# Two token tiles per step in the gated recurrences of a three-branch mixer, one core

## The chip, the cores and the metric

The kernel runs on one core of a Trainium2 chip. It computes a two-layer model in float32: 256 context tokens and 2,048 latent tokens of width 1,024 go through two layers, each with an input projection, three groups of heads side by side and an output projection. The metric is the device time of one execution in microseconds (us). TensorE (PE in the profile) multiplies, VectorE (DVE) works elementwise, ScalarE (ACT) evaluates functions and copies, GpSimd (POOL) has a few small steps, and SyncE (SP) issues most DMAs. PEld rows are TensorE's weight loads, which overlap its multiplications.

## The reference, cut to what matters

The change lies in the gated recurrences (heads of groups A and C). Per head a state `S` of key width by value width is carried over the tokens, forwards and backwards, in chunks of 64 tokens:

```python
CHUNK = 64
def step(s, inp):                       # one chunk, all heads
    qc, kc, vc, gc = inp
    b = jnp.cumsum(gc, axis=2)          # log decay from the chunk's start
    diff = b[:, :, :, None, :] - b[:, :, None, :, :]
    decay = jnp.where(lower, jnp.exp(jnp.where(lower, diff, 0.0)), 0.0)
    scores = jnp.einsum('bhid,bhjd,bhijd->bhij', qc, kc, decay)
    o = (jnp.einsum('bhij,bhjv->bhiv', scores, vc)
         + jnp.einsum('bhid,bhdv->bhiv', qc * jnp.exp(b), s))
    b_end = b[:, :, -1:, :]
    s = (s * jnp.exp(b_end[:, :, 0, :])[..., None]
         + jnp.einsum('bhjd,bhjv->bhdv', kc * jnp.exp(b_end - b), vc))
    return s, o
...
o_lf, _ = scan_dir(lat, 0, s_cf)        # forwards, from the context's final state
o_lb, _ = scan_dir(lat, 1, s_cb)        # backwards
return o_lf + o_lb, o_ctx
```

Group A has 4 heads with 64 keys, group C 4 heads with 32 keys; all values are 64 wide. Group B is latent attention with 4 heads over all 2,304 tokens. The outputs of the three groups are gated, joined and projected; the second layer needs no context output.

## The kernel before

The program is laid out by a scheduler that takes the operations in the order in which the Python code writes them as their priority and fixes, ahead of time, one order of instructions for each engine. Tiles come from pools by tag; `bufs` says how many buffers a tag has, and a new tile of a tag waits until the oldest is no longer read.

Each layer has three stages. `project` (to about 700 us in the first layer, from about 1,800 to 2,620 us in the second) multiplies the normed tokens with twelve groups of weights and stores the results in DRAM: forget gates `F`, keys `K` and queries `Q` with the key dimension on partitions, values and gates in `nat` by token. `mix` (about 700 to 1,750 us and 2,620 to 3,640 us) holds the attention and the recurrences side by side. `output` projects.

In `mix`, two generators are advanced in turn. `attention` yields after each pair of heads of a 128-token tile. The recurrence has two sweeps over 18 tiles of 128 tokens: `back_states` goes backwards and stores the backward scan's state at each chunk's end in `sb`; `recur` goes forwards and makes the outputs. `mix` advances the recurrence in proportion to the attention done; a tile of `recur` counts as 2.5 tiles of `back_states`, and a tile is written out whole.

All heads lie in three blocks of 128 rows: two blocks of group A (64 rows per head) and one of group C (32 rows per head, four heads). `fa`, `ka` and `qs` hold decays, keys and queries of a tile for both directions. The scores of a chunk are worked out in levels: level -1 is the diagonal, and levels 0 to 5 join neighbouring runs of 1 to 32 tokens. For each level, ScalarE gathers the keys (`km`, L706), TensorE multiplies keys and queries (`pa`, L774), VectorE merges the result under a mask into `acc` (L779), and VectorE multiplies keys (`ka`, L716, L719) and queries (`qa`, L728, L739) by the decays of the neighbouring runs and joins the decays (`t`, L741).

`level_scores` gives TensorE 12 products per tile and level. Each uses 64 rows and 64 columns of the array, at position (0, 0) or (64, 64) in turn: eight of 64 moving columns (group A) and four of 128 (group C). Since a block of 64 rows holds two heads of group C, their queries are stored twice in `Q`, each copy with the other head's rows at zero (L474), so one product with 128 columns serves both heads. A product on 32-bit operands shows as two records in the trace.

`chunk_products` turns the keys (`pk`, L614), copies them (`kn`, L616) and multiplies by the values (`pub`, `puf`, L623), 16 products per tile into two PSUM tiles, one per chunk. `chunk_outputs` adds 48 products per tile into two PSUM tiles `po`, one per half of the heads (L790, L801), at four positions of 64 by 64 if both halves run together. All of `pa`, `pub`, `puf` and `po` share the PSUM tag `R` with two buffers of one bank each.

Of the kernel before, what the change touches and what calls it, by code (L numbers as in the profile page):

```python
# [7 lines left out]
F32 = mybir.dt.float32  # L8
# [8 lines left out]
P = 128  # L17
# [11 lines left out]
SEG = 128  # L29


def view(ap, offset, dims, parts=None):
    """A free-dimension pattern of its own on the tile behind ap."""
    pd = list(ap.ap[0])
    if parts is not None:
        pd[1] = parts
    return bass.AP(ap.tensor, ap.offset + offset, [pd] + [list(d) for d in dims])


class Route:  # L40
    """Tiles by tag, each from the pool that holds the tag: the order of pools is the order in memory."""
# [12 lines left out]
class Trunk:  # L54
    def __init__(self, ctx, tc, io, nlat):
# [5 lines left out]
        self.ntiles = self.nt // P  # L61
        self.cpool = ctx.enter_context(tc.tile_pool(name="cpool", bufs=1))
# [10 lines left out]
    def split(self, hi, lo, src, hi_eng="act", lo_eng="dve"):  # L73
        """src = hi + lo with both parts in the tensor engine's one-pass format."""
# [10 lines left out]
    def rsqrt(self, pool, v, n, name):  # L85
        """(v + eps already added) ** -0.5 for a [P, n] tile."""
# [4 lines left out]
    def constants(self):  # L91
# [3 lines left out]
        self.mhalf = c.tile([P, 8], F32, name="mhalf")  # L95
        nc.vector.memset(self.mhalf, -0.5)
        # the gated heads' query scale, on the rows of the even and of the odd heads
        self.hm = c.tile([P, 2], F32, name="hm")
        for r in range(4):
            for i in range(2):  # L100
                nc.vector.memset(self.hm[32 * r:32 * r + 32, i:i + 1], float(32.0 ** -0.5) if r % 2 == i else 0.0)
# [7 lines left out]
    def scratch(self, l):  # L109
        """Layer l's arrays in DRAM, and its modulation columns."""  # L110
# [5 lines left out]
        S["F"] = d.tile([P, self.ntiles, 2, 3, SEG], F32, name=f"dF{l}")  # L116
        S["K"] = d.tile([P, self.ntiles, 2, 3, SEG], F32, name=f"dK{l}")
        S["Q"] = d.tile([P, self.ntiles, 4 * SEG], F32, name=f"dQ{l}")
# [4 lines left out]
        S["sb"] = d.tile([P, self.ntiles, 2, 3, 64], F32, name=f"dsb{l}")  # L123
# [12 lines left out]
    def mod_first(self, S, R, ps, first):  # L136
        """Layer 0's shift and scale as columns."""
# [23 lines left out]
    def mod_rest(self, S0, S1, R, bm0):  # L161
        """Layer 0's gate and layer 1's modulation: products along the free dimension, one column block at a time."""
# [41 lines left out]
    def lower_bounds(self, S):  # L204
        """Layer 1's forget-gate floor: the running sum of the softmax over layers less its first term."""
# [20 lines left out]
    def gate_weights(self, l, S, R):  # L226
        """The low-rank gate weights stacked [hi; hi; lo], against gates stacked [hi; lo; hi]."""
# [9 lines left out]
    def latent_weights(self, l, S, R, ps):  # L237
        """The low-rank query and key weights joined: M_h = W_uq,h W_uk,h^T; and the rotary and value ones."""
# [38 lines left out]
            # the first two weight groups run side by side while the first block's tokens come in  # L277
# [59 lines left out]
    # weight groups in the order in which they run: first column, number of columns  # L337
# [17 lines left out]
    def normed_pair(self, l, S, R, ps, pr, plain=False):  # L355
        """The modulated norm of two token tiles, transposed: [d, k, 256]; plain leaves out the modulation."""
# [47 lines left out]
    def group(self, l, S, R, ps, g, w, h, pairs):  # L404
        """One weight group against a block's token pairs; yields after each pair."""
# [4 lines left out]
        def natural(pr):  # L410
            """[P, tile of the pair, 256]: tokens on partitions, n weight columns."""
# [9 lines left out]
        def transposed(pr):  # L421
            """[P, 128-column block, 256]: weight columns on partitions, the pair's tokens."""
# [12 lines left out]
        def by_tile(o):  # L435
# [758 lines left out]
```

## Time and profile before

| | us |
|---|---|
| median of 3 runs | 3836.99 |
| lowest and highest | 3836.19, 3838.03 |
| span of the profiled execution | 3840.8 |
| TensorE busy in it | 3740.7 (97%) |
| VectorE busy | 2529.3 (66%) |
| ScalarE busy | 1452.2 (38%) |

The page gives each engine's busy time, its busy share in 40 slices, and the granted clock of TensorE. A matmul's row shows how long it was in the array, and matmuls overlap, so the busy time of PE says only that something was in flight; what a piece of work costs PE is read from the starts of the rows: the start of the next piece less its own. The timeline of an engine merges neighbouring rows of one line, with the count behind the x.

### The profile page before, as it was taken

How to read it: one execution, taken by the hardware profiler on the slowest of the kernel's cores; microseconds unless marked ns; L12 is line 12 of the kernel's file. 1: busy time of each engine (PE TensorE's matmuls, PEld its weight loads, DVE VectorE, ACT ScalarE, POOL GpSimd, SP SyncE). 2: the span in 40 equal slices, each digit the busy share in tenths (PEclk: the TensorE clock that was granted, in tenths of full speed). 3: DMA queues.
4: the chain of work that ended last, by engine and by line, in shares of the span. 5: the costliest groups of instructions: out<-in, count | busy, mean ns of one | idle time of the engine just before them, and what ended most of it. 6: DMA issues, size and time to landing. Idle time of an engine off the chain costs nothing.

```text
span 3840.8 us, 82784 instructions
## 1 busy us (share of the span) xinstructions
PE 3740.7 (97%) x34152; PEld 3341.4 (87%) x34152; DVE 2529.3 (66%) x6956; ACT 1452.2 (38%) x2347; POOL 187.3 (5%) x194
## 2 busy tenths in 40 slices
PE   8899999999999999998999999999999999999899
PEld 5899999888888888887879999998888888888777
DVE  6763242577888888776765432426778888888566
ACT  3524242344444444442115252523444444444400
POOL 1000000000000000010110000000000000000111
PEclk9999999999999999999999999999999999999999
DMA  7775453323222212114435453523231212211232
GB/s 253 229 206 155 122 155 108 110 85 92 76 68 62 69 57 69 54 59 167 150 105 181 141 156 101 170 90 118 78 96 49 79 55 69 73 55 33 89 140 104
DMA packets 305850, 415.30 MB, mean 108 GB/s; under 512 B 43008, under 2 KB 235840, under 8 KB 304448
## 3 DMA queue, kind: packets, MB, share of 16 engines
q1 hardware_dynamic: 304032, 407.64, 33.8%
q8 instruction: 269, 4.41, 0.5%
q10 hardware_dynamic: 1440, 2.36, 0.2%
q14 instruction: 109, 0.89, 0.1%
HBM read 290.89 MB, written 119.03 MB: 107 GB/s over the span
## 4 chain that ended last, share of the span: by engine, by line
PE 71%; DVE 2%; DMA 2%; ACT 1%; issue 0%; POOL 0%; SPq 0%; DVEq 0%; ACTq 0%; POOLq 0%
PE pj L417 10%; PE pa L774 7%; PE ptp L924 6%; PE pj L428 5%; PE oc L917 4%; PE oc L913 4%; PE pzo L1069 3%; PE pzo L1070 3%; PE pzo L1071 3%; PE pss L888 3%; PE oc L914 3%; PE pss L889 3%; PE pss L891 3%; PE pss L890 3%; PE pss L892 3%; PE po L801 1%
## 5 line engine op out<-in xcount | busy, mean ns | idle before, releaser
L417 PE MATMUL pj<-wh,hl 128*128 128x256 f32 (+1 forms) x2224 | 623.0, 281 | 8.4 <-DVE hl L83 8.4
L417 PE MATMUL pj<-wh,hh 128*128 128x256 f32 (+1 forms) x2224 | 624.5, 281 | 2.0 <-DVE ve L369 1.2
L417 PE MATMUL pj<-wl,hh 128*128 128x256 f32 (+1 forms) x2224 | 623.1, 280 | 0.0
L77 ACT CAST ph<-ptp 128x512 fp32r<-128x512 f32 x580 | 333.2, 586 | 369.9 <-PE ptp L924 349.6
L83 DVE TENSOR_TENSOR pl<-ptp,ph 128x512 fp32r<-128x512 f32 x580 | 392.9, 686 | 111.2 <-ACT ph L77 109.9
L893 DVE TENSOR_SCALAR_CACHE_REDUCE sx<-pss 128x512 f32<-128x512 f32 (+1 forms) x648 | 399.2, 631 | 79.5 <-PE pss L892 74.2
L417 PEld LDWEIGHTS pj<-wh,hl 128*128 128x128 f32 x2224 | 421.5, 190 | 9.3 <-DVE hl L83 9.3
L417 PEld LDWEIGHTS pj<-wh,hh 128*128 128x128 f32 x2224 | 423.1, 190 | 2.7 <-DVE ve L369 1.6
L417 PEld LDWEIGHTS pj<-wl,hh 128*128 128x128 f32 x2224 | 422.3, 190 | 0.0
L924 PE MATMUL ptp<-ident,sx 128*128 128x128 f32 x2320 | 368.5, 275 | 17.2 <-ACT sx L903 17.2
L903 ACT ACTIVATE sx<-sx,nm 128x2304 f32<-128x2304 f32 (+1 forms) x136 | 288.4, 2121 | 173.5 <-DVE nm L899 171.4
L913 PE MATMUL oc<-ph,cnh 128*128 128x256 f32 x1160 | 346.0, 320 | 5.1 <-ACT ph L77 4.4
L83 DVE TENSOR_TENSOR wl<-wraw,wh 128x1024 fp32r<-128x1024 f32 (+1 forms) x144 | 169.6, 1211 | 238.8 <-ACT wh L77 238.7
L428 PE MATMUL pj<-hh,wh 128*128 128x256 f32 x1136 | 321.0, 283 | 0.0
L428 PE MATMUL pj<-hh,wl 128*128 128x256 f32 x1136 | 319.3, 281 | 0.0
L428 PE MATMUL pj<-hl,wh 128*128 128x256 f32 x1136 | 318.2, 280 | 0.0
L914 PE MATMUL oc<-ph,cnl 128*128 128x256 f32 x1160 | 301.9, 282 | 0.0
L924 PEld LDWEIGHTS ptp<-ident,sx 128*128 128x128 f32 x2320 | 272.8, 141 | 28.0 <-ACT sx L903 19.4
L774 PE MATMUL pa<-qa,km 64*64 64x64 f32 (+1 forms) x4896 | 279.3, 248 | 3.4 <-DVE qa L739 3.1
L888 PE MATMUL pss<-cth,qh 128*128 128x512 f32 (+1 forms) x648 | 269.4, 416 | 5.4 <-DVE sx L893 5.0
L917 PE MATMUL oc<-pl,cnh 128*128 128x256 f32 x1160 | 251.1, 297 | 7.0 <-DVE pl L83 6.8
L774 PEld LDWEIGHTS pa<-qa,km 64*64 64x64 f32 x4896 | 202.4, 134 | 58.4 <-issue 34.3
(241 smaller groups left out, 8035.7 us busy)
## 6 DMA issues: line engine op xcount, KB each, us to landing
wraw<-in_w_in_dram SPq DMA_DIRECT2D x132, 512.0 KB, 4.7
dnat<-stg SPq DMA_DIRECT2D x104, 256.0 KB, 2.1
vg<-dnat SPq DMA_DIRECT2D x34, 512.0 KB, 4.2
yt<-dy SPq DMA_DIRECT2D x34, 512.0 KB, 3.6
wmt<-in_w_modT_dram SPq DMA_DIRECT2D x64, 256.0 KB, 4.0
fa<-dF SPq DMA_DIRECT2D x36, 384.0 KB, 3.3
ka<-dK SPq DMA_DIRECT2D x36, 384.0 KB, 3.3
dK<-stg SPq DMA_DIRECT2D x36, 256.0 KB, 4.1
```

The source lines that it names most:

```text
L77: nc.scalar.copy(hi, src)
L83: nc.vector.tensor_tensor(lo, src, hi, op=ALU.subtract)
L417: nc.tensor.matmul(pj[:, j, :n], h[pr][a][:, k, tk], w[b][:, k, :n], start=(k == 0 and a + b == 0), stop=(k == KD - 1 and a == 1))
L428: nc.tensor.matmul(pj[:, j, :], w[b][:, k, cs], h[pr][a][:, k, :], start=(k == 0 and a + b == 0), stop=(k == KD - 1 and b == 1))
L774: nc.tensor.matmul(pa[rows, po:po + n], km[rows, sl, tk:tk + 64], mv, start=True, stop=True, tile_position=(64 * e, 64 * e))
L888: nc.tensor.matmul(pss[:, :n], G["qh"][hp][:, i, tk], K["cth"][:, ks], start=True, stop=False)
L893: nc.vector.tensor_scalar(sx[:, ks], pss[:, :n], SCALE, None, op0=ALU.mult, op1=ALU.max, accum_out=mx[:, nb:nb + 1])
L903: nc.scalar.activation(sx[:, :nk], sx[:, :nk], AF.Exp, bias=nm, accum_out=sm)
L913: nc.tensor.matmul(oc, K["cnh"][:, ks], ph[:, c, :], start=(kc + c == 0), stop=False)
L914: nc.tensor.matmul(oc, K["cnl"][:, ks], ph[:, c, :], start=False, stop=False)
L917: nc.tensor.matmul(oc, K["cnh"][:, ks], pl[:, c, :], start=False, stop=(kc + c == nch - 1))
L924: nc.tensor.transpose(pt[:, c, i, :], pexp[i][:, (kc + c) * P:(kc + c + 1) * P], self.ident)
```

## The change

Every step of the recurrences takes two token tiles (a pair, 256 tokens, four chunks). `F`, `K`, `Q` and `sb` are stored by pairs. The directions in `F` change places, so that one vector instruction per level reaches both directions: `qa` is made by one product instead of four, and each level's products on `qa` by one instruction instead of four to six. `ka`, `t`, the merge and the sums cover 256 tokens. Tags that had two buffers (`fa`, `ka`, `vg`, `qs`, `acc`, `v2`, and in the attention `ym`) have one of twice the size; `R` is one PSUM tile of two banks. `Q` holds group C's queries once, scaled; the copies with zeros, `qm`, are made by ScalarE just before the outputs. In `level_scores` the products of group C use 32 rows at positions (0, 0), (64, 64), (32, 0) and (96, 64) with 64 moving columns; group A's products of a level come first, then group C's. `recur` yields after each level, an eighth of 2.5 each time.

```diff
-SEG = 128
+SEG = 256
+NCH = SEG // 64
...
             elif g == 5:
-                o, o2 = stage(), stage()
-                for i in range(2):
-                    nc.scalar.mul(view(o[:], 64 * i, [[SEG, 4], [1, 64]]),
-                                  pj[:, 0].rearrange("p (c n) -> p c n", n=64), self.hm[:, i:i + 1])
-                nc.sync.dma_start(out=S["Q"][:, tt, 2 * SEG:4 * SEG], in_=o)
-                nc.scalar.copy(o2[:, 1], pj[:, 1])
+                o = stage()
+                nc.scalar.mul(o[:, 0], pj[:, 0], float(32.0 ** -0.5))
+                nc.scalar.copy(o[:, 1], pj[:, 1])
+                nc.sync.dma_start(out=S["Q"][:, pr, 2, :], in_=o[:, 0])
...
+    def chunk_products(self, rp, rps, kT, vt):
+        nc = self.nc
+        kn = rp.tile([P, 2, 3 * P], F32, tag="km", bufs=2, name="kn")
+        for j in range(2):
+            pk = rps.tile([P, 3, P], F32, tag="mi", name="pk")
+            for b in range(3):
+                nc.tensor.transpose(pk[:, b, :], kT[:, b, j * P:(j + 1) * P], self.ident)
+            nc.scalar.copy(kn[:, j], pk.rearrange("p b n -> p (b n)"))
+        pu = rps.tile([P, 2, 512], F32, tag="R", name="pu")
+        for j in range(2):
+            for s in range(4):
+                for e, c in ((0, 0), (1, 1), (1, 0), (0, 1)):
+                    ksl, rows, blk, vb = self.head_rows(4 * e + s)
+                    cs = slice(64 * c, 64 * c + 64)
+                    o = 192 * j + 64 * blk
+                    nc.tensor.matmul(pu[rows, c, o:o + 64], kn[cs, j, ksl], vt[cs, j, vb * 64:vb * 64 + 64],
+                                     start=True, stop=True, tile_position=(64 * c, rows.start))
+        return pu[:, :, 0:384].rearrange("p c (j n) -> p c j n", j=2)
+
+    def advance(self, to, st, tt, ch, pu):
         for b in range(3):
...
+            self.nc.vector.scalar_tensor_tensor(
+                out=to[:, b, :], in0=st[:, b, :], scalar=tt[:, b, ch:ch + 1],
+                in1=pu[:, ch % 2, ch // 2, b * 64:b * 64 + 64], op0=ALU.mult, op1=ALU.add)
...
+                qa = rp.tile([P, 2, L3], F32, tag="qa", name="qa")
+                nc.vector.tensor_tensor(qa, qs.rearrange("p b n -> p (b n)").unsqueeze(1).to_broadcast([P, 2, L3]),
+                                        fa.rearrange("p d b n -> p d (b n)"), op=ALU.mult)
...
+                if need:
+                    km = rp.tile([P, 3, SEG], F32, tag="km", bufs=2, name="km")
+                    for d in range(2):
+                        blk = [[2 * c, nb], [1, c]]
+                        nc.scalar.copy(view(km[:], c * d, blk), view(kap, L3 - d * (L3 - c), blk))
+                    self.level_scores(rps, km, qa, c, lv, acc)
...
                 if need:
-                    # d = 0: suffix products of the backward decays; d = 1: prefix products of the forward ones
-                    qap = qa[:]
-                    nq = SEG // (2 * c)
-                    for d in range(2):
-                        q0 = d * (L4 + c)
-                        tb = lt + 1 if d == 0 else 0
-                        qv = view(qap, q0, [[2 * c, 2 * nq], [1, c]])
-                        nc.vector.tensor_tensor(qv, qv, view(tap, tb, [[2, 2 * nq], [0, c]]), op=ALU.mult)
...
-                        for pt in parts:
-                            qv = view(qap, q0 + pt[0], pt[1:4])
-                            nc.vector.tensor_tensor(qv, qv, view(tap, tb + pt[4], pt[5:8]), op=ALU.mult)
...
+                    qv = view(qa[:], 0, [[2 * c, nb], [L3 + c, 2], [1, c]])
+                    nc.vector.tensor_tensor(qv, qv, view(tap, 1, [[2, nb], [lt - 1, 2], [0, c]]), op=ALU.mult)
...
+                if need:
+                    yield 2.5 / 8
...
     def level_scores(self, rps, km, q, c, lv, acc):
...
-        pa = rps.tile([P, 512], F32, tag="R", bufs=2, name="pa")
...
+        pa = rps.tile([P, 2, 512], F32, tag="R", name="pa")
+        todo = []
+        for ch in range(NCH):
+            tk = slice(64 * ch, 64 * ch + 64)
+            for sl in range(4):
+                n, b = (64, sl) if sl < 2 else (32, 2)
                 for e in range(2):
...
+                    r = 64 * e if sl < 2 else 64 * e + 32 * (sl - 2)
+                    rows = slice(r, r + n)
...
+                    po = 128 * ch + 64 * (sl // 2)
+                    todo.append((sl // 2, pa[64 * e:64 * e + 64, sl % 2, po:po + 64], km[rows, b, tk], mv, (r, 64 * e)))
+        for part in range(2):
+            for g, out, w, mv, pos in todo:
+                if g == part:
+                    nc.tensor.matmul(out, w, mv, start=True, stop=True, tile_position=pos)
...
     def chunk_outputs(self, S, rp, rps, p, acc, qa, v2, vt, sbt, sts):
...
+        qm = []
+        for i in range(2):
+            m = rp.tile([P, 2, SEG], F32, tag="km", bufs=2, name="qm")
+            nc.scalar.mul(m, qa.rearrange("p d (b n) -> p d b n", b=3)[:, :, 2], self.hm[:, i:i + 1])
+            qm.append(m)
+        po = rps.tile([P, 2, 512], F32, tag="R", name="po")
...
-            total = self.ntiles * (1 + self.PACE)
+            total = self.npairs * 3.5
```

First place: TensorE, outputs of one step of `recur` in the first layer. `po` are the output products, `puf` chunk products, `ptp` and `oc` attention. Before:

```order
L924 MATMUL ptp<-ident,sx 128x128 x6
L623 MATMUL puf<-vg,kn 64x64 x4
L623 MATMUL puf<-vg,kn 32x64 x4
L790 MATMUL po<-v_12886,acc 64x64 x8
L801 MATMUL po<-sbt,qa 64x64 x2
L801 MATMUL po<-stf,qa 64x64 x2
```

After:

```order
L914 MATMUL oc<-ph,cnl 128x256
L789 MATMUL po<-v_12044,acc 64x64 x32
L801 MATMUL po<-sbt,qa 64x64 x4
L801 MATMUL po<-stc,qa 64x64
```

Where a tile's outputs came in two halves of 24 products with attention between them, a pair's 96 products stand in one row.

Second place: TensorE, one level's product `pa` among attention (`pss`, `oc`, `ptp`, `poa`) in the first layer. Before:

```order
L924 MATMUL ptp<-ident,sx 128x128 x6
L774 MATMUL pa<-qs,ksum 64x64 x8
L774 MATMUL pa<-qs,ksum 64x128 x4
L892 MATMUL pss<-ks,rl 128x512
L888 MATMUL pss<-cth,qh 128x512
```

After, one product whole, and one in pieces:

```order
L936 MATMUL poa<-uv_1137,os 128x128 x2
L765 MATMUL pa<-qa,km 64x64 x32
L888 MATMUL pss<-cth,qh 128x512
L889 MATMUL pss<-ctl,qh 128x512
```

```order
L765 MATMUL pa<-qa,km 64x64 x13
L917 MATMUL oc<-pl,cnh 128x256 x2
L765 MATMUL pa<-qa,km 64x64 x7
L888 MATMUL pss<-cth,qh 128x512
```

A tile's 12 products have become a pair's 32, all of 64 columns, and there are half as many levels; some are still cut by attention products.

Third place: VectorE, one level in the first layer (`qa`, `ka`: queries and keys; `acc`: the merge; `pl`, `sx`: attention). Before:

```order
L728 TENSOR_TENSOR qa<-qa,t_17143 128x64x2
L739 TENSOR_TENSOR qa<-qa,t_17143 128x32x2
L779 COPY_PREDICATED acc<-mask,pa 128x512
L739 TENSOR_TENSOR qa<-qa,t_17143 128x32x2 x3
L716 TENSOR_TENSOR ka<-ka,t_17193 128x24x2x8
```

After:

```order
L769 COPY_PREDICATED acc<-mask,pa 128x1024
L724 TENSOR_TENSOR qa<-qa,t_17926 128x48x2x8
L717 TENSOR_TENSOR ka<-ka,t_18008 128x24x2x16
L893 TENSOR_SCALAR sx,mx<-pss 128x512
L85 TENSOR_TENSOR pl<-ptp,ph 128x512
```

The merge of a pair now comes first, then one product on `qa`; `ka` runs two levels ahead.

## Rows read from the trace of the kernel before

**Rows 1.** The page: busy us, share, instructions; granted clock in 40 slices.

```profile
PE 3740.7 (97%) x34152; PEld 3341.4 (87%) x34152; DVE 2529.3 (66%) x6956; ACT 1452.2 (38%) x2347; POOL 187.3 (5%) x194
PEclk9999999999999999999999999999999999999999
```

**Rows 2.** Windows, both mixes: us, busy us of each engine, clock, DMA, GB/s.

```profile
700.00:1700.00 1000.00, 983.58 (x10706) 837.87 (x10705) 815.26 (x2628) 432.74 (x694) 31.20 (x34) 1.00 0.24 72
2620.00:3600.00 980.00, 965.46 (x10199) 825.88 (x10199) 786.26 (x2513) 428.58 (x667) 34.69 (x33) 1.00 0.23 70
```

**Rows 3.** Waits of PE, whole span: us in total, times, longest.

```profile
PE oc L917 <- DVE pl L83: 6.8, 14, 1.6
...
PE pa L774 <- DVE qa L739: 3.1, 3, 2.4
```

**Rows 4.** Timeline of PE, one level product: start, us, what, count [idle before].

```profile
931.70 0.40 PE L917 MATMUL oc<-pl,cnh 128*128 128x256 f32 x2
932.03 1.12 PE L774 MATMUL pa<-qs,ksum 64*64 64x64 f32 x24
933.08 0.39 PE L838 MATMUL pq<-cqh,mh 128*128 128x256 f32 x1
933.30 0.28 PE L838 MATMUL pq<-cql,mh 128*128 128x256 f32 x1
933.42 0.27 PE L838 MATMUL pq<-cqh,ml 128*128 128x256 f32 x1
```

**Rows 5.** Timeline of PE, outputs of one tile, both halves together.

```profile
1223.59 0.40 PE L917 MATMUL oc<-pl,cnh 128*128 128x256 f32 x2
1223.83 0.49 PE L924 MATMUL ptp<-ident,sx 128*128 128x128 f32 x3
1224.25 0.70 PE L790 MATMUL po<-v,acc 64*64 64x64 f32 x32
...
1225.58 0.30 PE L801 MATMUL po<-stf,qa 64*64 64x64 f32 x8
1225.82 0.33 PE L924 MATMUL ptp<-ident,sx 128*128 128x128 f32 x1
```

**Rows 6.** Timeline of PE, outputs of one tile, one half alone.

```profile
1291.94 0.68 PE L790 MATMUL po<-v,acc 64*64 64x64 f32 x16
...
1293.49 0.39 PE L913 MATMUL oc<-ph,cnh 128*128 128x256 f32 x1
```

**Rows 7.** Timeline of PE, chunk products of one tile, whole, then one half.

```profile
907.38 0.73 PE L623 MATMUL pub<-bv,kn 64*64 64x64 f32 x32
908.04 0.55 PE L614 MATMUL pk<-ident,bk 128*128 128x128 f32 x3
...
910.82 0.69 PE L623 MATMUL pub<-bv,kn 64*64 64x64 f32 x16
911.44 0.39 PE L913 MATMUL oc<-ph,cnh 128*128 128x256 f32 x1
```

**Rows 8.** The page's groups: level products 0 to 5 (count, busy, mean ns, idle).

```profile
L774 PE MATMUL pa<-qa,km 64*64 64x64 f32 (+1 forms) x4896 | 279.3, 248 | 3.4 <-DVE qa L739 3.1
```

**Rows 9.** Groups of VectorE by form: busy us, mean ns of one, idle before.

```profile
L779 DVE COPY_PREDICATED acc<-mask,pa 128x512 f32<-128x512 uint8 x204 | 150.4, 737 | 13.5 <-PE pa L774 12.9
L739 DVE TENSOR_TENSOR qa<-qa,t 128x64 f32<-128x64 f32 x544 | 96.4, 219 | 0.9 <-PE pa L774 0.8
L728 DVE TENSOR_TENSOR qa<-qa,t 128x128 f32<-128x128 f32 x340 | 85.0, 287 | 16.1 <-PE pa L774 15.3
L716 DVE TENSOR_TENSOR ka<-ka,t 128x384 f32<-128x384 f32 x136 | 75.4, 554 | 13.4 <-ACT km L706 13.2
...
L716 DVE TENSOR_TENSOR ka<-ka,fa 128x384 f32<-128x384 f32 x34 | 29.5, 869 | 0.0
```

**Rows 10.** Timeline of PE, a level product that waits.

```profile
945.03 1.12 PE L774 MATMUL pa<-qa,km 64*64 64x64 f32 x24 [2.36 <-DVE qa L739]
```

**Rows 11.** The page's DMA issues: count, KB each, median us to landing.

```profile
ka<-dK SPq DMA_DIRECT2D x36, 384.0 KB, 3.3
```

More of the change, by code (lines that the diff above doesn't have):

```diff
@@ L691, in recur @@
                 ksum = rp.tile([P, 3, SEG], F32, tag="km", bufs=2, name="ksum")
                 nc.vector.tensor_tensor(ksum, ka[:, 0], ka[:, 1], op=ALU.add)
-                acc = rp.tile([P, 512], F32, tag="acc", bufs=2, name="acc")
-                v2 = rp.tile([P, 2, 256], F32, tag="v2", bufs=2, name="v2")
-                for e in range(2):
-                    nc.sync.dma_start(out=v2[64 * e:64 * e + 64],
-                                      in_=S["nat"][tk, 256 * e:256 * e + 256].rearrange("(c j) n -> j c n", c=2))
@@ L698, in recur @@
[L698 to L710 removed]
+                acc = rp.tile([P, 2, 512], F32, tag="acc", name="acc")
@@ L711, in recur @@
+                self.level_scores(rps, ksum, qs, 1, -1, acc)
+                yield 2.5 / 8
+            ta = fa
+            for lv in range(6):
+                c = 1 << lv
                 nb = L3 // (2 * c)
@@ L784, in chunk_outputs @@
+    def chunk_outputs(self, S, rp, rps, p, acc, qa, v2, vt, sbt, sts):
         nc = self.nc
-        po = [rps.tile([P, 256], F32, tag="R", bufs=2, name="po") for _ in range(2)]
-        quads = ((0, 0), (1, 1), (1, 0), (0, 1))
-        for sl in range(4):
-            for e, c in quads:
-                rows = slice(64 * e, 64 * e + 64)
-                nc.tensor.matmul(po[e][64 * c:64 * c + 64, sl * 64:sl * 64 + 64],
-                                 acc[rows, c * 256 + sl * 64:c * 256 + sl * 64 + 64],
-                                 v2[rows, c, sl * 64:sl * 64 + 64], start=(sl == 0), stop=False,
-                                 skip_group_check=True, tile_position=(64 * e, 64 * c))
@@ L804, in chunk_outputs @@
-        o = rp.tile([P, 512], F32, tag="o", bufs=2, name="o")
-        for e in range(2):
-            nc.scalar.copy(o[:, e * 256:e * 256 + 256], po[e])
-        sq = rp.tile([P, 512], F32, tag="sq", name="sq")
-        nc.scalar.activation(sq, o, AF.Square)
-        ss = rp.tile([P, 8], F32, tag="rss", bufs=2, name="rss")
+                    o = 256 * j + 64 * sl
+                    oa = 128 * (2 * j + c) + 64 * (sl // 2)
+                    nc.tensor.matmul(po[64 * c:64 * c + 64, e, o:o + 64], acc[rows, sl % 2, oa:oa + 64],
+                                     v2[rows, 2 * j + c, sl * 64:sl * 64 + 64], start=(j == 0 and sl == 0), stop=False,
+                                     skip_group_check=True, tile_position=(64 * e, 64 * c))
@@ new lines, in chunk_outputs @@
+        for j in range(2):
+            for sl in range(4):
+                for d in range(2):
+                    for e, c in quads:
+                        rows = slice(64 * e, 64 * e + 64)
+                        ch, b, o = 2 * j + c, min(sl, 2), 256 * j + 64 * sl
+                        tk = slice(64 * ch, 64 * ch + 64)
+                        q = qm[sl - 2][rows, d, tk] if sl > 1 else qa[rows, d, sl * SEG + 64 * ch:sl * SEG + 64 * ch + 64]
+                        sv = sbt[rows, ch, b, :] if d == 0 else sts[ch][rows, b, :]
+                        nc.tensor.matmul(po[64 * c:64 * c + 64, e, o:o + 64], q, sv, start=False,
+                                         stop=(d == 1 and sl == 3 and j == 1), skip_group_check=True,
+                                         tile_position=(64 * e, 64 * c))
@@ L819, in query_group @@
+        nc.sync.dma_start(out=self.pair_rows(S["y"], p, 0, 512), in_=o)
     def query_group(self, S, ap, aps, t):
@@ L1096 @@
     CHEAP = 0.3
-    PACE = 2.5
     EARLY = 1000
```

269 lines of the change are left out of this document (110 added, 159 removed).

## The prediction

> **What bounds the kernel now.** I read the page first. TensorE is busy for 97% of the span, VectorE for 66%, ScalarE for 38%, and the granted clock is 1.00, the 2.4 GHz level, in all slices that do work [rows 1]. The share alone says little, since matmuls overlap, so the windows come next: in the steady part of both mixes TensorE has something in flight for 98% of the time, at clock 1.00, and VectorE works for 80 to 82% [rows 2]. Last come the waits. The only ones that TensorE has on the recurrence in any number are three of 3.1 us in all, and on the attention's subtraction `pl` 14 of 6.8 us [rows 3]. So the mixes are bound by TensorE's stream. An edit is worth what it takes out of that stream, and VectorE's saved time is worth nothing until TensorE waits for it. The change can therefore gain in one way (a recurrence that costs TensorE less) and lose in one (a longer chain from VectorE back to TensorE).
>
> **Prices of TensorE's small tiles.** They come from starts, not durations. One level product has 24 records: 16 of 64 columns and 8 of 128, which is 32 widths of 64. In [rows 4] its first record starts at 932.03 and the next line at 933.08, so it takes 1.05 us, with two array positions in turn. Half a tile's outputs (48 records of 64) takes 1293.49 - 1291.94 = 1.55 us, also with two positions [rows 6]. The difference, 0.50 us for 16 widths, is **31 ns per width with two positions**, and 1.05 - 32 x 0.031 leaves 0.06 us for the batch itself. All 96 records at four positions take 1225.82 - 1224.25 = 1.57 us [rows 5], so (1.57 - 0.06) / 96 = **15.7 ns per width with four positions**. A change between full tiles and small ones costs something too. Two `oc` records take 0.33 us ahead of a small batch [rows 4] and 0.24 ahead of full ones [rows 5]: 0.09 to enter. The record behind a small batch takes 0.22 instead of the 0.12 of its kind (933.08 to 933.30 and to 933.42 [rows 4]): 0.10 to leave. **A batch costs 0.19 us beside its own time.** The chunk products fit the prices: whole, 32 records take 908.04 - 907.38 = 0.66 us, and half of them 911.44 - 910.82 = 0.62 [rows 7]. For the whole batch 32 x 0.0157 + 0.06 = 0.56, so 0.10 is left, which I put on the change of tile height inside it (64 to 32 rows).
>
> **The change on TensorE, term by term.**
>
> Level products. [rows 8] has 4,896 records, so 34 tiles by 6 levels by 24; with the diagonal there are 34 x 7 = 238 products, and 17 x 7 = 119 for pairs. Two tiles cost 2 x 1.05 = 2.10 us now. For a pair, group A has 32 records at two positions, 32 x 0.031 = 0.99; group C has 32 records that may run at four positions, 32 x 0.0157 = 0.50; with 0.06 for the batch and 0.10 for the change of height that is 1.65. No row shows a level product with tiles of 32 rows. The bounds of group C's half are 0.50 and 0.99, and I take 0.50, because in the outputs [rows 5] four positions of which two share their columns already run at that price. 119 x 0.45 = **-53 us**.
>
> Batches. Counting small tiles that follow one another as one batch, the trace of before has 452 and the new order has 338: 114 x 0.19 = **-22 us**.
>
> Outputs. Of 34 tiles 16 have them whole and 18 in halves: 16 x 1.57 + 18 x 3.10 = 81 us. After, all 17 pairs have one run of 192: 17 x (192 x 0.0157 + 0.06) = 52. **-29 us**.
>
> Chunk products. There are 72 now (18 tiles in each layer and sweep); 44 are whole and 28 in halves: 44 x 0.66 + 28 x 1.24 = 64 us. After there are 36 of twice the size, and at most the whole price for each half of one: 72 x 0.66 = 48. **-16 us**.
>
> Cut products. Attention cuts 98 of the 238 level products now, and 59 of 119 in the new order. Their entering and leaving is in the batches; beyond that a piece may leave a position idle. If a cut costs 14 widths of 0.031 us more than now in each of the 59, that is +26 us, and as much less is as possible. I take 0 and keep +-26 for the range.
>
> **The change on VectorE and the chain back.** VectorE's products have one price: 64 elements 219 ns, 128 elements 287, 384 elements 554 [rows 9], so about 150 ns and 1.05 ns per element. The new merge has 1,024 elements. Its bounds are one and two of today's 737 ns; I take 737 + 512 x 1.05 = 1.27 us. The new `qa` product has 768: 150 + 768 x 1.05 = 0.95 us (bounds 0.55 and 1.11; with the pattern of level 0, which takes 869 ns for 384, up to 1.74). In all VectorE loses instructions; that is hidden by the same stream of TensorE that hides them today, and its value is 0.
>
> What does count is that `R` now is one PSUM tile. The next level's product starts only when the merge has read the last one, and when `qa` is multiplied, and the order puts these behind one another: 1.27 + 0.95, with 0.27 for the last record's way through the array [rows 4] and half a microsecond for an attention operation that VectorE has just begun, about 3.0 us. Behind a waiting product stands all of the attention, since TensorE's order is fixed. Today the same wait exists and costs up to 2.36 us in a place [rows 10], but rarely, as two tiles of `R` let the merge lag. From the new order, with the times of the rows above, I added up the attention that lies between one level's product and the next: 102 steps, median 3.4 us, mean 4.0, fifteen of them under 2.0. The part of the chain that is not covered sums to 17 us for a chain of 2.6, 29 for 3.2, 82 for 4.0, 124 for 4.6 and 157 for 5.0. For 3.0 I take **+25 us**.
>
> **At nothing.** ScalarE makes two `qm` per pair more and copies the same keys; it is at 43% in the mixes [rows 2]. SyncE issues fewer transfers. `fa`, `ka` and `vg` have one buffer now, so the next pair's loads start when this pair is through with them: 768 KB for `fa` and `ka`, by 3.3 us for 384 KB [rows 11] 6.6 us. In the new order 10 to 45 us of other products lie between a pair's last level and the next pair's first, which covers it; if that cover were gone, 17 x 5 = 85 us would be the most. The projection has the same matmuls and drops one stored segment of `Q`. The recurrence still ends about two attention steps ahead of the attention, so no tail appears.
>
> **Sum.** -53 - 22 - 29 - 16 + 25 = -95 us. On the profiled execution's 3840.8 that is 3745.8; the profiled execution lies 3.8 us above the median of the runs, so the median should be **about 3740**.
>
> **Rivals.** *Only two of the 32-row products run at a time.* Two of the four positions share an output bank of `pa` in different rows of the array; should that, or tiles of 32 rows, stop them from overlapping, group C costs 31 ns per width: 119 x 32 x 0.0153 = +58 us, 3798. For it speaks that no row has this tile; against it that today's two positions, which also write one bank, already overlap at 31 ns a width [rows 4] and would otherwise need twice that. The Trainium skill, "TensorEngine Tiling (Array Packing)", section "Restrictions and Gotchas", Gotcha 1, says that tiles in different rows of the array cannot use the same PSUM bank at the same time. By it today's level product would take about 2.05 us where the trace has 1.05, so here the trace disagrees with it for tiles that write different partitions, and no run shows it for 32 rows. Chance 0.18.
>
> *The chain becomes the bound, and the kernel is slower.* Place: between `pa` of one level and of the next, where VectorE's attention operations (a `copy_predicated` of 512 elements, 737 ns, is about their size [rows 9]) get between merge and `qa`, two or three of them each time, and the chain is 5.0 us. Price 157 instead of 25: 3740 + 132 = 3872. It decides from a chain of 4.6 us, where 124 us eat the whole gain of 120. For it speaks that VectorE is the second busiest engine in the mixes [rows 2]; against it that the order has merge and `qa` behind one another in most steps and that VectorE gets idler. Chance 0.09.
>
> *No change.* A chain between 4.4 and 4.6: 0.03. *A deeper gain*: cuts at -26 and the chain well covered, 17 us or less: 3705; chance 0.07.
>
> **How the numbers follow.** The forecast, 3740, has the remaining 0.63, with a range of its own of 3710 to 3770 (cuts +-26, merge and `qa` at their bounds). The range of 3703 to 3800 adds the rival of the 32-row tiles and the deeper gain, and leaves the slower and unchanged cases and some edges out. A measurement of this kernel tells about 0.2%, 7.7 us, from no change. Faster: 0.63 + 0.18 + 0.07 = 0.88; same 0.03; slower 0.09.
>
> **What would show it.** Starts of `pa`: a whole batch of 64 records 1.65 us long, its second half 0.5 against 1.0 for the first; 2.15 in all would show the first rival. 192 records of `po` in 3.07 us. Some 340 small batches. A steady VectorE share well under 80%. In the waits of TensorE, `pa` on `acc` or `qa` with some 25 us; over 120 there would prove the second rival, and waits of `pa` on a load or on `fa` would show that single buffers are not free. If all four terms are there and the time is not, the recurrence no longer fits beside the attention, and the gap is a tail at the end of a mix.

## The result and the profile after

The changed kernel takes 3866.34 us (median of three runs, 3866.07 to 3869.9) against 3836.99: 1.0075 of the time before, 95% interval 1.0057 to 1.0093. It is slower by 29 us where the prediction had 97 us faster. The profiled execution's span is 3864.6 us. The page's busy times and granted clock:

```profile
PE 3665.0 (95%) x36056; PEld 3309.4 (86%) x36056; DVE 2418.7 (63%) x5430; ACT 1437.7 (37%) x2296; POOL 185.3 (5%) x159
PEclk9999999999999999998999999999999999999999
```

TensorE is in use for 76 us less than in [rows 1] and VectorE for 111 us less, yet the span is longer: the work went down and the waiting went up. The windows of both mixes show it (us, busy us of PE, PEld, DVE, ACT, POOL, granted clock, DMA share, GB/s); the same windows before are [rows 2]:

```profile
700.00:1700.00 1000.00, 939.10 (x11507) 817.38 (x11507) 751.83 (x1813) 426.64 (x674) 28.55 (x19) 0.98 0.22 69
2620.00:3600.00 980.00, 920.31 (x11039) 801.25 (x11039) 729.19 (x1772) 416.04 (x642) 28.56 (x19) 0.98 0.22 67
```

TensorE was in use for 983.58 and 965.46 us there and is for 939.10 and 920.31 now, and the mean clock fell from 1.00 to 0.98. What TensorE waits for (total, times, longest; what answers to [rows 3]):

```profile
PE oc L917 <- DVE pl L85: 51.7, 31, 4.7
PE pss L888 <- DVE sx L893: 22.2, 21, 3.8
PE oc L913 <- ACT ph L79: 21.9, 22, 2.3
...
PE pa L765 <- DVE qa L724: 12.3, 16, 2.8
```

The first three are the attention's instructions: its products on `pl` and `ph`, and its scores `pss`, which need VectorE to have read the last ones (`sx`). Before, they waited 6.8 us [rows 3] and

```profile
PE pss L888 <- DVE sx L893: 5.0, 7, 1.5
PE oc L913 <- ACT ph L77: 4.4, 6, 1.5
```

The recurrence's own product `pa`, on which the prediction had set its 25 us, waits 12.3 for `qa`.

Adding up TensorE from each record's start to the next record's start (or to its own end, if nothing follows at once), over both mixes, gives the account. The third kernel is run r5 below, the fourth r15.

| us in both mixes, rounded | before | after | one tile, r5 | pairs, work left out, r15 |
|---|---|---|---|---|
| recurrence (`pa`, `po`, `pu`) | 445 | 344 | 358 | 362 |
| attention (`pss`, `oc`, `ptp`, `poa`) | 1470 | 1493 | 1464 | 1486 |
| other products | 109 | 111 | 107 | 109 |
| idle | 46 | 141 | 41 | 79 |
| sum | 2070 | 2089 | 1970 | 2035 |

So the recurrence gave back 101 us, idle time took 95 of them, the attention's own records took 23 more, and the other stages 5. (r5's sum is 119 us under that of the changed kernel; another 18 us between these two lie outside the mixes, and no run looks into those.)

**The terms on TensorE came out.** A whole level product of a pair, and the one of r5 for one tile (timelines of TensorE: start, us, what, count):

```profile
1427.34 1.77 PE L765 MATMUL pa<-qa,km 64*64 64x64 f32 x64 [0.39 <-DVE qa L724]
1429.04 0.50 PE L888 MATMUL pss<-cth,qh 128*128 128x512 f32 x1
```

```profile
986.56 1.07 PE L773 MATMUL pa<-qa,km 64*64 64x64 f32 x32
987.56 0.38 PE L896 MATMUL pss<-cth,qh 128*128 128x256 f32 x1
```

From start to next start that is 1.70 us for a pair (1.65 was forecast, 2 x 1.05 before) and 1.00 for a tile. The 16 widths of each group between the two cost 0.70. The single records in the trace show how: in the first part two records start 7 to 36 ns apart, in the second four within 20 ns, and in both the next such set follows 58 ns after the last. That is 29 ns per width in group A and 15 in group C, and 8 x 58 + 4 x 58 ns is the 0.70.

**Where the idle time arises.** At the end of a pair, VectorE, ScalarE and TensorE of the changed kernel:

```profile
1303.92 1.11 DVE L726 TENSOR_TENSOR t<-t 128x192 f32<-128x192 f32 x4
1305.63 1.23 DVE L814 TENSOR_TENSOR o<-o,rrs 128x1024 f32<-128x1024 f32 x1 [0.59 <-POOL rrs L90]
1306.89 1.23 DVE L815 TENSOR_TENSOR o<-o,vg 128x1024 f32<-128x1024 f32 x1
1308.03 0.95 DVE L717 TENSOR_TENSOR ka<-ka,t 128x768 f32<-128x768 f32 x1
1308.90 0.69 DVE L85 TENSOR_TENSOR pl<-ptp,ph 128x512 fp32r<-128x512 f32 x1
```

```profile
1304.46 0.59 ACT L79 CAST ph<-ptp 128x512 fp32r<-128x512 f32 x1 [0.94 <-PE ptp L924]
```

```profile
1304.62 0.28 PE L914 MATMUL oc<-ph,cnl 128*128 128x256 f32 x1
1309.64 0.79 PE L917 MATMUL oc<-pl,cnh 128*128 128x256 f32 x2 [4.74 <-DVE pl L85]
1310.23 0.41 PE L924 MATMUL ptp<-ident,sx 128*128 128x128 f32 x1
...
1310.66 0.41 PE L914 MATMUL oc<-ph,cnl 128*128 128x256 f32 x1
```

`ph` is there at 1305.05, so `pl` could start. In VectorE's fixed order the products with the norm and with the gates (L814, which waits another 0.59 us for GpSimd's power, and L815) and the next pair's `ka` stand in front of it: 3.85 us from 1305.05 until `pl` starts at 1308.90. TensorE's order has nothing between the products on `ph` and those on `pl`, so it stands still for 4.74 us.

**What a wait costs beyond itself.** Behind it, L914 takes 0.41 us instead of 0.28. The window names the clock:

```profile
1309.60:1313.00 3.40, 3.36 (x11) 2.98 (x12) 1.80 (x5) 1.01 (x1) 0.00 (x0) 0.50 1.01 312
1320.00:1330.00 10.00, 9.58 (x170) 8.56 (x169) 9.97 (x22) 5.64 (x9) 0.00 (x0) 1.00 0.41 134
```

0.50 is the lower level, 1.2 GHz. In the mixes of the changed kernel 20 stretches of 2 to 9 us have records of the longer kind, 85 us in all, against 7 with 28 us before. At half the pace 57 us more of it cost up to 29 us. By the granted clock, 80 us of the attention's own time lie at 0.50, against 24 before; half of the 56 us more is 28, so the clock is all of the attention's 23 us, and without it the attention would take some 5 us less than before.

### The profile page after: what moved, and what is told of

The parts are those of the page before. It is cut to its first block, busy times and chain, and to the rows that moved or that the text cites. A ratio compares the mean times of both kernels' runs of the same rounds, so it can differ in the third digit from the quotient of the medians.

```text
span 3864.6 us, 84193 instructions
## 1 busy us (share of the span) xinstructions
PE 3665.0 (95%) x36056; PEld 3309.4 (86%) x36056; DVE 2418.7 (63%) x5430; ACT 1437.7 (37%) x2296; POOL 185.3 (5%) x159
## 4 chain that ended last, share of the span: by engine, by line
PE 46%; DVE 5%; DMA 2%; issue 1%; POOL 1%; ACT 1%; SPq 0%; DVEq 0%; ACTq 0%; POOLq 0%
PE pj L420 10%; PE pj L431 5%; PE pzo L1070 3%; PE pzo L1071 3%; PE pzo L1072 3%; PE ptp L924 3%; PE pa L765 2%; PE oc L917 2%; PE pss L888 2%; PE oc L913 2%; PE pss L889 1%; PE pss L890 1%; PE pss L891 1%; PE pss L892 1%; PE oc L914 1%
## 5 line engine op out<-in xcount | busy, mean ns | idle before, releaser
L914 PE MATMUL oc<-ph,cnl 128*128 128x256 f32 x1160 | 306.7, 286 | 0.0
L913 PEld LDWEIGHTS oc<-ph,cnh 128*128 128x128 f32 x1160 | 225.3, 194 | 43.3 <-ACT ph L79 32.4
L917 PEld LDWEIGHTS oc<-pl,cnh 128*128 128x128 f32 x1160 | 188.1, 194 | 80.2 <-DVE pl L85 64.5
```

Source lines behind the costliest of these rows:

```text
L913: nc.tensor.matmul(oc, K["cnh"][:, ks], ph[:, c, :], start=(kc + c == 0), stop=False)
L914: nc.tensor.matmul(oc, K["cnl"][:, ks], ph[:, c, :], start=False, stop=False)
L917: nc.tensor.matmul(oc, K["cnh"][:, ks], pl[:, c, :], start=False, stop=(kc + c == nch - 1))
```

## The experiments

Each changes the changed kernel unless said otherwise. Idle time is TensorE's in both mixes (before 46, after 141); a batch is a row of small tiles without attention between them. Every edit gives the scheduler another order, so a run moves more than the one thing that it names; where it matters, the number of batches tells.

**One tile per step (r1, r5, r8).** The lines that set it:

```diff
-SEG = 256
+SEG = 128
...
-            fa = rp.tile([P, 2, 3, SEG], F32, tag="fa", name="fa")
+            fa = rp.tile([P, 2, 3, SEG], F32, tag="fa", bufs=2, name="fa")
...
-        for p in range(self.npairs):
+        for p in range(self.ntiles // NJ):
```

`NJ` is 1; `F`, `K`, `Q` and `sb` are stored by tiles again, and `ka`, `vg`, `qs`, `acc`, `v2` and `ym` get two buffers like `fa`.

> The changed kernel with one tile of 128 tokens per step instead of two, and with the double buffers of before (fa, ka, vg, qs, acc, v2, ym); all else of the change stays: one qa instruction for both directions, 32-row tiles, R as one tile of two banks, qm by ScalarE, a pause after each level. Theory (the loss is the size of the work that VectorE gets in one go for a pair, in front of the attention's subtraction): TensorE keeps -34 us on level products (238 x 0.14), -28 on outputs and -16 on chunk products against before, its idle time in the two mixes falls from 140 us to about 50, and the time is 3765 to 3790. Rival (the loss comes with the single R tile or with one chained qa instruction per level): the idle time stays over 100 us and the time is 3830 or more.

Measured: 3830.35 us, 0.9984 (0.9974 to 0.9994), with 107 us of idle time: the theory's time was missed, and by its numbers the rival would have held. But the waits on `pl` were gone (7.3 us), and two new ones stood at the top of the list:

```profile
PE pty L1058 <- DMA yt<-dy: 65.9, 2, 33.8
PE pq L846 <- ACT cqh L80: 34.4, 2, 17.4
```

Both lie at the borders of stages, where buffers of the next stage take the place of the last one's. The smaller pool of the recurrence had shifted all that lies behind it by 2,632 words. r5 fills the pool up to the size it has before:

```diff
+            pad = rp.tile([P, 2632], F32, name="pad")
+            nc.gpsimd.memset(pad[:, 0:1], 0.0)
             self.reset = rp.tile([P, SEG], F32, name="reset")
```

> The version with one tile per step, with 2,632 unused words per partition in the recurrence's pool, so that all later buffers lie where they lie in the kernel before. Theory: the waits of 17 us at the start of each mix (pq on cqh) and of 33 us at the start of each output stage (pty on the load of yt), which that version alone had, come from buffers that moved onto others that are still in use; with them gone about 90 us of its 3830 go: 3735 to 3760, TensorE's idle time in the mixes about 45 us as in the kernel before, against 141 us with pairs. Rival (those waits come from a recurrence that ends too late or loads that queue): they stay, 3820 to 3835.

Measured: 3727.21 us, 0.9712 (0.9698 to 0.9727), faster than both kernels. Those two waits are gone, so the position of the buffers was worth 103 us, and idle time is 41 us. The changed kernel has neither wait (1.0 us on the load of `yt`, none on `cqh`), so its own loss is another. The page of r5, and its waits that answer to the three above:

```profile
PE 3641.4 (98%) x36056; PEld 3277.1 (88%) x36056; DVE 2449.6 (66%) x6042; ACT 1487.0 (40%) x2603; POOL 185.9 (5%) x196
```

```profile
PE oc L925 <- DVE pl L86: 13.1, 17, 1.7
...
PE oc L921 <- ACT ph L80: 6.5, 13, 2.1
...
PE pss L896 <- DVE sx L901: 3.5, 6, 1.0
```

`R` as one tile, the 32-row products, one `qa` product for both directions, `qm` and the pauses after each level are all in r5. None of them is the loss; it comes with the pairs and with what they force. r8 takes the pauses back to one per tile:

```diff
-                if need:
-                    yield 2.5 / 8
```

> One tile per step, double buffers, pool filled up, and one pause per tile as in the kernel before instead of one after each level. Theory: a tile's work in one go is what before had too, so within 15 us of the version with pauses after each level, with more cut level products. Rival (the pauses after each level make the gain): 20 us or more slower.

Measured: 3764.81 us, 0.9809 (0.9793 to 0.9825), 38 us behind r5: the expected 15 were too few. Idle time is the same (42), but level products are cut more (447 small batches against 376), and `pa` takes 15 us more; 17 of the 38 lie outside the mixes, and their cause stays open. The pauses help.

**One pause per pair (r4).** The same edit on pairs.

> The changed kernel with one pause per pair, as before had one per tile, instead of one after each level. Theory (size of the work in one go): the same or slower, 0 to +30 us, with more idle time of TensorE. Rival (the pauses after each level, which string the recurrence out along the attention, are the loss): 15 to 40 us faster.

Measured: 3876.68 us, 1.0100 (1.0085 to 1.0115), 10 us slower, as the theory had it, but for another reason: idle time fell to 109, and `pa` grew by 33 us since 486 batches stand where 338 did. Both runs give the price of a cut in `pa`: 15 / 71 and 33 / 148, about 0.22 us.

**Two positions instead of four for group C (r2).**

```diff
-        for part in range(2):
+        for part in range(3):
             for g, out, w, mv, pos in todo:
-                if g == part:
+                if (g if pos[0] in (0, 64) else 2) == part:
```

> The changed kernel, only the order of group C's products in a level is changed: all products at positions (0,0) and (64,64) first, then all at (32,0) and (96,64), so that two positions alternate instead of four. If four positions overlap as the prediction said, a whole level product grows by 0.5 us from 1.70 to 2.2, 58 us in 119. If TensorE's stream still sets the time where it does not wait, the kernel slows by 35 to 60 us; if the waits swallow such work, by under 20 us. If the four positions brought nothing, no change at all.

```profile
1506.13 2.05 PE L765 MATMUL pa<-qa,km 64*64 64x64 f32 x64
1508.12 0.39 PE L913 MATMUL oc<-ph,cnh 128*128 128x256 f32 x1
```

Measured: 3888.36 us, 1.0132 (1.0117 to 1.0147), 22 us slower, and 1.98 us per product (1508.12 - 1506.13) instead of 1.70. Four positions overlap, so the first rival falls; but two cost only 0.28 us more, not 0.50. `pa` grew by 34 us and idle time fell by 6: between the two bounds that were set, work on TensorE is still paid for in good part. The single records show why it isn't 0.50: each position still starts a record every 58 ns, but the first products at (32, 0) and (96, 64) start while some at (0, 0) and (64, 64) are still to come, so the two halves ran side by side for a part. They also show tiles of 32 rows at (0, 0) and (64, 64), which write one PSUM bank, starting 7 ns apart, which no row had shown before the change.

**Single buffers with one tile (r6, r10, r11).** The change put `o` into `acc`'s tag, where before it had two buffers of its own, and `sq` into `t0`'s (L804, L806). r6 is one tile per step with the change's single buffers (`ym` alone keeps two); r10 moves `o` out of `acc`'s buffer (`o = vt[:, :, 0:512]`); r11 has double buffers, but `acc` has one that `o` shares, and `sq` lies in `t0`'s. In all three the pool is filled up.

> The same with one tile per step, but with the single buffers of the change (fa, ka, vg, qs, acc, v2; sq shares a buffer with t0, o with acc), and the pool filled up to the size of before. If the loss of the change is the amount of VectorE's work per pair, single buffers cost little: within 20 us of the version with double buffers, idle time under 70 us. Rival (single buffers tie the start of a step to the end of the last one): 40 us or more slower than with double buffers.

> One tile per step with the single buffers, but o in the value half of vg. Theory B: most of the 112 us between single and double buffers is the sharing of acc and o, so 60 us or more come back, 3780 or less, and the wait of 59 us at the start of the output stages goes with it. If the single loads (fa, ka, vg, qs, v2) are the cause: under 25 us come back.

> The counterpart: one tile per step with double buffers for fa, ka, vg, qs, v2 and ym, but one buffer for acc that o shares, and sq in t0's. Theory B: this alone loses most of the 112 us, 3800 or more against 3727. If the single loads are the cause, it stays below 3750.

Measured: r6 3841.63 us (1.0011, 1.0002 to 1.0020), r10 3760.81 (0.9793, 0.9777 to 0.9808), r11 3815.81 (0.9938, 0.9920 to 0.9956). Single buffers cost 114 us at one tile, and sharing `acc` with `o` most of it: 81 come back when it is undone, 89 are lost when it is done alone (with `sq` in `t0`'s buffer). The other single buffers are the 34 us between r5 and r10. The rival of r6 held. ScalarE's waits in r6 and r11, and TensorE's in r6:

```profile
ACT acc L775 <- DMA dy<-o: 44.8, 20, 4.9
```

```profile
ACT acc L775 <- DMA dy<-o: 38.1, 18, 4.5
```

```profile
PE pty L1060 <- DMA yt<-dy: 58.8, 2, 30.1
```

`acc` of the next step is written by ScalarE (L775), which must wait until `o` has been stored; the next step's first levels stand behind that, and ScalarE's `ph` too. The output stages then wait some 30 us each for the load of what was stored last, 59 of r6's 154 us of idle time; r10 and the changed kernel lack this wait.

**The same with pairs (r9).** In the changed kernel the same wait stands, 9 times:

```profile
ACT acc L767 <- DMA dy<-o: 27.3, 9, 6.9
```

```diff
-        o = rp.tile([P, 2, 512], F32, tag="acc", name="o")
+        o = vt[:, :, 0:512]
```

> The changed kernel (pairs), but the outputs o lie in the value half of vg, which is through by then, and not in acc's only buffer; nothing else is changed. With one tile per step single buffers cost 112 us, and in the changed kernel ScalarE waits nine times, 27 us, for the store of o before it may write the next pair's acc, with the attention's ph behind it. Theory B (that shared buffer is the main loss of the pairs): TensorE's idle time in the mixes falls from 141 to 80 us or less, and the kernel is 40 us or more faster, below 3825. Theory A (the amount of VectorE's work in a row at a pair's end): idle time stays above 115 us, the kernel gains under 20 us.

Measured: 3863.44 us, 1.0061 (1.0043 to 1.0079): nothing gained, idle time 128. Theory B falls for pairs. The wait went, and the one on `pl` halved, but that on `qa` took its place:

```profile
PE pa L765 <- DVE qa L724: 27.2, 25, 2.8
PE oc L916 <- DVE pl L85: 25.2, 25, 2.8
```

Idle time fell by 13 us, and `pa` grew by 12, since 396 batches stand where 338 did. Nor is `o` free of every tie now: the load of the next values into `vg` waits for its store (SyncE, 31.7 us in 13 places).

**VectorE's work (r7, r3, r13, r12).** r7 cuts the long instructions in two; r3 leaves out the norm of the outputs (L806 to L814), r13 the level products on `qa` (L724); r12 takes one tile per step in `back_states` alone.

```diff
-            nc.vector.copy_predicated(acc.rearrange("p e (s i) -> p (e s) i", i=64),
...
+            for e in range(2):
+                nc.vector.copy_predicated(acc[:, e].rearrange("p (s i) -> p s i", i=64),
```

> The changed kernel with two tiles per step, but VectorE's long instructions (merge, qa, ka, the two on o) cut into two of half the length; the order of TensorE's work is written as before. Some 27 instructions more per pair of about 0.15 us each: 65 us more of VectorE's time. If the length of a single instruction is what the attention waits for, idle time falls by 40 us or more and the kernel is faster by 20 us or more in spite of it. If it is the amount of the recurrence's work that stands in a row, the idle time stays within 20 us and the kernel is the same or slower.

> The changed kernel without the norm of the recurrence's outputs (square, sum, power on GpSimd and the multiplication by it are left out; the gate stays). Theory (VectorE's work at a pair's end blocks the attention's subtraction): the waits of 2.6 to 4.7 us of oc on pl at the ends of pairs go, 32 pair ends x 0.7 to 1.3 us = 20 to 40 us of TensorE's idle time, and the kernel is 20 to 45 us faster. Rival (the waits come from anywhere VectorE is busy, the norm is one place among many and the next work moves up): under 12 us faster.

> The changed kernel without the level products on qa (their output is not the reference's: queries keep the decay of one token; TensorE's work is unchanged). This takes 16 x 6 x 2 instructions of 0.95 us off VectorE, 180 us, and the step from the merge to the next product out of the chain. Theory A: idle time in the forward sweep falls by 30 to 50 us of the 99, the kernel gains 30 to 60. Rival (the chain through merge and qa is covered as forecast and only the pairs' ends matter): under 15 us.

> The changed kernel with pairs in the forward sweep, but one tile per step in the sweep for the backward states (half-length scans, six state steps in a row instead of twelve). In the changed kernel TensorE is idle for 42 us of the two stretches in which this sweep runs, against 17 before, and VectorE is at stb, stc and bpe then. Theory A (VectorE's work in a row): the idle time of these stretches falls to 15 to 25 us and the kernel gains 15 to 30. Rival (single buffers or loads at the start of a mix): under 8 us.

Measured: r7 3861.19 us (1.0064, 1.0049 to 1.0079), idle time 141: the length of an instruction is not it. r3 3829.85 (0.9983, 0.9974 to 0.9993): 36 us, 29 of them idle time, in the expected range. r13 3847.71 (1.0028, 1.0018 to 1.0037): 19 us, 16 of them idle time, between the 30 of theory A and the 15 of its rival. r12 3865.53 (1.0065, 1.0048 to 1.0082; its trace is of the fastest execution, 3852.16): nothing; the idle time of the state sweep fell only from 42 to 36 us, and theory A's number for it was wrong.

The rival of r12, the single buffers of the loads, can be read from the runs with one tile per step. TensorE's idle time in the two stretches of this sweep (from the start of a mix to its first `pa`) is 13 us in r5 and in r11, which have two buffers for the loads, 30 in r10, which has one, and 36 in r12. VectorE's scan `bpe` waits there for the load of its decays (r5, then r10):

```profile
DVE bpe L659 <- DMA bf<-dF: 1.2, 2, 0.8
DVE bpe L659 <- DMA bf<-dF: 16.5, 16, 2.0
```

In r12 it is 21.8 us in 18 places, and 6.9 in 4 in the changed kernel. So the smaller step brought out the wait for the load, and r12 can't tell what VectorE's work in a row costs in this sweep.

**All of it together (r14, r15, r16).** r14 joins r3, r12 and r13; r15 adds the place of `o` from r9; r16 joins r3 and r9.

> Both of the last and the norm left out as well: one tile per step in the state sweep, no level products on qa, no norm of the outputs (the output is not the reference's). If VectorE's work in a row is the whole loss, the idle time in the mixes comes down to that of the kernel before, about 46 us or less, and the time to the forecast 3740 or below. If something else of the pairs costs as well, it stays above 3775.

> As the run without norm, without level products on qa and with one tile per step in the state sweep (the output is not the reference's), and the gated outputs lie in the value half of vg instead of acc's buffer. That run kept 92 us of idle time and 26 us in which ScalarE waits for the store of o, with the attention's ph behind it. If that wait is what is left, idle time falls to 65 us or less and the time to 3795 or less. If it is the single buffers of the loads or the pairs' other work, the idle time stays above 80.

> The changed kernel without the norm (the output is not the reference's) and with o in the value half of vg. Alone the first took 29 us of idle time and 34 us, the second 13 us of idle time and nothing. If they are two separate losses, they add: idle time about 100, 3820 to 3830. If the wait for o's store is one loss with two ends, more than the sum comes back: idle under 85, 3805 or less.

Measured: r14 3820.6 us (0.9958, 0.9941 to 0.9975), idle time 92; r15 3815.92 (0.9946, 0.9929 to 0.9962), idle 79; r16 3827.15 (0.9971, 0.9961 to 0.9981), idle 104. r16 lies where the sum of its two parts puts it (104 us of idle time against 141 - 29 - 13 = 99), so nothing more comes back when both are undone; in time the buffer of `o` is no loss that the runs can tell from nothing (3 us). r15's 79 us are next to the 80 that stood for "not that wait". Idle time adds up roughly (29 for the norm, 13 for `o`'s buffer, 16 for `qa`), and r14 stays above the 3775 that was set for "something else costs as well". The longest row that remains in r14 names the same instruction:

```profile
PE oc L905 <- DVE pl L85: 31.6, 29, 3.4
```

## Why the prediction was wrong

Point by point, by its own steps:

- **TensorE's terms: right, but for the batches.** Level products -53 forecast, -50 measured; outputs -29 and -31; chunk products -16 and -19. The four positions overlap. The small batches are 338, as counted, but their 22 us did not come: in r5, with 76 batches fewer than before, the attention's own time fell by 6 us, 0.08 each, and in the changed kernel by some 5 once the clock is taken out. The cuts, which the sum had at 0, cost 0.22 us each in `pa`.
- **The chain through merge and `qa`: in place, at half its size.** +25 us were taken, and `pa` waits 12.3 us for `qa`. The second rival had its place here. Its 3872 us are close to the 3866 that were measured, but that is luck: its sign, over 120 us of waits of `pa`, is not there.
- **"VectorE loses instructions", with the value 0: this step failed.** It counted VectorE's sum and the recurrence's own wait, and all its signs on waits ask for `pa`. It left out that the attention's `pl`, `sx` and, through ScalarE, `ph` stand in the same fixed queue behind whatever the recurrence has there, and that a pair puts twice as much in a row. TensorE's waits on them went from 16 us to 96. A busy share that falls (from 82% to 75% and from 80% to 74%) says nothing on that.
- **"At nothing" for the single buffers: this failed too, by omission.** The loads were weighed and `acc` was not, though the change gives `o` `acc`'s only buffer. With one tile per step this sharing costs 81 to 89 us. With pairs the wait is there (27 us of ScalarE), but undoing it alone brings nothing. The loads were weighed for the forward sweep only; in the state sweep the single buffer costs 17 us of idle time with one tile per step (r10 against r5).
- **The clock was left out.** [rows 2] had it at 1.00 and [rows 1] says only 90% or more; TensorE hardly waited then. Behind the waits stand stretches at 1.2 GHz, 57 us more of them.

What is settled: the loss comes with pairs and their buffers, not with the rest of the change, as r5 has the rest and is 2.9% faster than before. Between r5 and the changed kernel lie 139 us. With `o` out of `acc`'s buffer, r10 and r9 differ by the step: 3761 us for tiles, 3863 for pairs. (They differ in `ym`'s buffers too, two and one, but no trace of the pairs has a wait of over 0.8 us for `ym` to be stored.) So the other single buffers are 34 us, the pairs 103 and the shared buffer 3. The losses overlap: on the way through r6 the single buffers are 114 us and the pairs 25. Of the pairs' part are shown: the norm at a pair's end 36 us, the products on `qa` 19.

What stays open: r15 leaves the norm, the products on `qa`, the pairs in the state sweep and the shared buffer out, and is still 89 us slower than r5. In the traces 38 us of it are idle time, 22 the attention's, at a lower clock, and 18 lie outside the mixes. Of the 38, 23 are in the state sweep (36 against 13), where both take one tile per step and r15 has single buffers; r10, which in this sweep differs from r5 by the buffers alone, has 17 more than r5 there. The rest has no run of its own, and with pairs a second set of buffers was not tried.

## What to carry to other kernels

Where one engine bounds a stage and another serves two streams in one fixed order, count for each edit how much work it puts in a row in front of the other stream's instructions, and compare it with how far that stream runs ahead; the engine's busy share does not tell. When a step is made larger and buffers are halved for it, look at each shared buffer for the transfer that must end before the next step's first write. And when a pool changes its size, look at the first waits of the next stage: here 2,632 unused words were worth 103 us. When one wait is taken away and no time comes back, look for the one that it covered before calling it harmless: in r9 and r12 another grew in its place.

## What the runs showed of the hardware

After 4.74 us without work TensorE ran at a granted clock of 0.50 for some 5 us, and the changed kernel had 20 stretches at this level, 85 us. The Trainium skill, "TensorE: Matmul & The Clock Gate", Part 1, says that the slow level is the default and that activity releases it. The trace agrees, with 0.50 right behind the wait and 1.00 from 1320 on.

GpSimd's power took 1.64 us for 8 columns before and 3.38 us on average for 16 after, so joining two of them into one instruction saved nothing. Four array positions with tiles of 32 rows overlap at 15 ns per 64 columns, about as those of the outputs with tiles of 64 rows do (15.7 [rows 5]). Two positions that write different partitions of one PSUM bank start 7 ns apart in r2 and take 29 ns per 64 columns.
